# Rope tables on GpSimd, and a mixer's first chunks cut down to what the scan reads

## The chip, the cores and the metric

One core of a Trainium2 chip runs the whole program in one launch. The metric is the device time of one execution in microseconds (us). The kernel before takes 1905.51 us, the median of 3 runs (1904.94 to 1906.81). A change counts as seen here from about 0.2% on, 3.8 us.

## What is computed

A decoder trunk of two layers over 512 positions, width 1024, in float32. Each layer has a mixer, cross-attention into 256 memory tokens, and a gated MLP with a short convolution. Only the mixer's head matters here:

```python
h = rmsnorm(x, norm_mix[i])
z, xbc, dt_raw, c_q, c_kv, k_rope = jnp.split(h @ w_in[i], IN_SPLITS, axis=-1)
xbc = jax.nn.silu(causal_dwconv(xbc, ssm_conv_w[i], ssm_conv_b[i]))   # width 4
dt = jax.nn.softplus(dt_raw + dt_bias[i])                              # 16 heads
y = ssd_scan(xs, dt, a, bm, cm) + xs * d_skip[i][:, None]              # needs cumsum(dt * a)
q = rmsnorm(c_q, q_norm) @ w_uq ;  q_pe = apply_rope(q[..., 64:], cos, sin)
kv = rmsnorm(c_kv, kv_norm) @ w_ukv ;  k_pe = apply_rope(k_rope, cos, sin)
```

The tables are the cosine and sine of position times inverse frequency, the same for both layers.

## The kernel before

Activations lie transposed, features on the 128 partitions and the 512 positions along the row. Each float32 product is three matmuls of rounded halves (high by high, high by low, low by high; lines 168 to 170 in `mm3`). A weight tile of 128x1024 is loaded by SyncE into `wraw`; ScalarE rounds it to `whi` (line 107) and, as a rule, GpSimd subtracts to get `wlo` (line 108). There are three buffers of each, and the pair is made two tiles ahead. One **chunk** is 24 matmuls against one such pair: one column block of 128 features of a projection.

The mixer of a layer begins with six chunks (`latent_q`, `latent_kv`, and one that holds dt and the rope keys, `dtk`). A short run of 128x64 steps on VectorE (lines 415 to 430) makes the softplus `dt` and `w`, which is dt times a. Then 24 chunks follow in four groups of six (`inproj`), and attention's chunks. A loop gives each chunk a position, 0 to 23 for `inproj`. After each one, it takes a step of three coroutines:

- `front()`, the head: `rq` and `rk`, reciprocal roots of the latent norms (`rstd_cols`: four transposes on TensorE, a reduction on VectorE, a power on GpSimd in line 273, a product on VectorE in line 275); in layer 0 `rope_tables()`; rope keys `kpe`; query scales `csqa`, `csqb` (transposes by `bcast`, line 282); the normed key latents `ckh`, `ckl`; then the cumulative sums `acs` (two matmuls, lines 460 and 461, copied to SBUF in line 462), their transpose on TensorE (line 470) and its way through DRAM, `scr`.
- `scans`, one `ssd(g)` for each group, which start at the positions 5, 10, 16 and 21 and read `scr`, `acs`, `dt`.
- `memory()`, from position 12.

An `inproj` chunk of the convolved kind is followed by these steps: VectorE scales the bank (line 485), ScalarE makes the last tap and bias (492), VectorE adds three taps (494, three times), ScalarE takes the tanh (495), VectorE finishes (496).

TensorE's instructions stand in the order in which the program is written. The order on the other engines is chosen when the kernel is built, by a list scheduler, and is fixed from then on: each engine takes its instructions strictly one after the other.

## Time and profile before

| what | value |
|---|---|
| median of 3 runs | 1905.51 us |
| the profiled execution, its own time | 1904.88 us |
| its span, first to last instruction | 1903.2 us |
| TensorE busy | 1867.0 us, 98% |
| VectorE, ScalarE, GpSimd busy | 1035.5, 950.2, 885.7 us |
| mean granted TensorE clock | 0.995 |

The span is what the trace covers; some 1.7 us of the execution's own time lie outside it. Busy time of TensorE is modelled and includes matmuls that run at half clock. With an engine at 98%, the interesting part is the other 2%: where it stands still, and what it waits for there.

### The profile page before, as it was taken

Reading aid. Unit: us, or ns where it says so; the run is one execution under the profiler, and the core shown is the slowest. Engines: PE = TensorE matmul, PEld = TensorE weight load, DVE = VectorE, ACT = ScalarE, POOL = GpSimd, SP = SyncE. Lnnn points to the kernel's source line nnn. Section 1 sums busy time; section 2 is a strip of 40 time slices with the busy share of each in tenths; the row PEclk is TensorE's granted clock in tenths of the full one; section 3 lists DMA queues with packets and bytes.
Section 4 is the critical chain, followed back from the end, with each engine's and each line's share of the span. In section 5 each row is a group of like instructions: output and inputs, shape, how many; then the busy total and the mean of one; then the engine's idle time right before and its main releaser. Section 6 shows DMA issues by size and latency. Waiting matters only on the chain.

```text
span 1903.2 us, 24916 instructions
## 1 busy us (share of the span) xinstructions
PE 1867.0 (98%) x9264; PEld 1572.9 (83%) x9264; DVE 1035.5 (54%) x1967; ACT 950.2 (50%) x1694; POOL 885.7 (47%) x563
## 2 busy tenths in 40 slices
PE   8799999999999999999999999999999999999998
PEld 6588889988888888888887888898888888888887
DVE  5867788843343555541138777887334445555312
ACT  5366588843345444433235557888334544444321
POOL 5345455655416444433354454555553354444232
PEclk9899999999999999999999999999999999999999
DMA  5233311232213322233223332113322122332322
GB/s 168 68 122 111 103 51 59 93 125 94 91 34 109 100 100 97 92 97 100 92 100 101 113 110 82 58 62 122 110 91 88 50 96 98 100 100 90 102 91 84
DMA packets 56025, 178.47 MB, mean 94 GB/s; under 512 B 6368, under 2 KB 9312, under 8 KB 55904
## 3 DMA queue, kind: packets, MB, share of 16 engines
q1 hardware_dynamic: 49984, 166.32, 26.4%
q10 hardware_dynamic: 5920, 10.55, 1.7%
q8 instruction: 73, 1.20, 0.3%
q14 instruction: 48, 0.39, 0.1%
HBM read 174.69 MB, written 2.16 MB: 93 GB/s over the span
## 4 chain that ended last, share of the span: by engine, by line
PE 93%; DVE 2%; issue 1%; ACT 1%; POOL 1%; DMA 1%; SPq 0%; POOLq 0%; DVEq 0%; ACTq 0%
PE ps L168 28%; PE ps L170 28%; PE ps L169 28%; PE ps L728 2%; PE ps L709 1%; PE ps L583 1%; POOL wlo L108 1%; PE ps L589 1%; PE ps L562 1%; ACT whi L107 0%; DVE u L162 0%; PE ps L932 0%; PE ps L519 0%; PE ps L515 0%; PE ps L731 0%
## 5 line engine op out<-in xcount | busy, mean ns | idle before, releaser
L108 POOL TENSOR_TENSOR wlo<-wraw,whi 128x1024 fp32r<-128x1024 f32 (+1 forms) x290 | 679.1, 2343 | 855.7 <-ACT whi L107 836.6
L168 PE MATMUL ps<-u,whi 128*128 128x512 f32 (+1 forms) x2326 | 898.7, 386 | 7.7 <-ACT whi L107 5.1
L170 PE MATMUL ps<-u,wlo 128*128 128x512 f32 (+1 forms) x2326 | 890.0, 383 | 0.8 <-POOL wlo L108 0.6
L169 PE MATMUL ps<-u,whi 128*128 128x512 f32 (+1 forms) x2326 | 889.7, 383 | 0.0
L107 ACT ACTIVATE whi<-wraw 128x1024 fp32r<-128x1024 f32 (+2 forms) x319 | 328.2, 1030 | 494.7 <-PE ps L169 391.3
L168 PEld LDWEIGHTS ps<-u,whi 128*128 128x128 f32 x2326 | 438.9, 189 | 90.8 <-ACT whi L107 5.1
L170 PEld LDWEIGHTS ps<-u,wlo 128*128 128x128 f32 x2326 | 438.7, 189 | 87.3 <-POOL wlo L108 1.4
L169 PEld LDWEIGHTS ps<-u,whi 128*128 128x128 f32 x2326 | 439.2, 189 | 82.0 <-DVE u L165 0.7
L162 DVE TENSOR_TENSOR u<-ps,u 128x512 fp32r<-128x512 f32 (+2 forms) x236 | 137.2, 612 | 105.4 <-ACT u L159 104.7
L159 ACT ACTIVATE u<-ps 128x512 fp32r<-128x512 f32 (+2 forms) x236 | 117.7, 540 | 120.7 <-DVE ps L1021 98.4
L1017 DVE SCALAR_TENSOR_TENSOR u<-ps,small,u 128x510 f32<-128x510 f32 (+1 forms) x176 | 131.3, 749 | 74.7 <-ACT u L1015 71.7
L1010 DVE TENSOR_TENSOR ps<-ps,u 128x512 f32<-128x512 f32 x88 | 61.4, 700 | 109.9 <-PE ps L170 101.6
L301 POOL TENSOR_TENSOR u<-u,u 128x512 f32<-128x512 f32 (+1 forms) x82 | 102.5, 1251 | 37.0 <-ACT u L300 29.5
L108 DVE TENSOR_TENSOR wlo<-wraw,whi 128x1024 fp32r<-128x1024 f32 (+1 forms) x29 | 32.5, 1119 | 139.5 <-ACT whi L107 139.5
L697 POOL TENSOR_SCALAR u<-u,rs 128x512 f32<-128x512 f32 (+3 forms) x128 | 66.8, 537 | 79.7 <-DVE rs L696 75.0
L849 DVE TENSOR_TENSOR ps<-ps,u 128x512 f32<-128x512 f32 x32 | 22.4, 699 | 99.1 <-PE ps L170 99.1
L695 ACT ACTIVATE u<-ps,nm 128x512 f32<-128x512 f32 (+3 forms) x128 | 66.3, 524 | 18.1 <-DVE nm L692 12.1
L168 PE MATMUL ps<-u,u 128*128 128x512 f32 (+1 forms) x224 | 73.1, 326 | 0.9 <-ACT u L695 0.9
L170 PE MATMUL ps<-u,u 128*128 128x512 f32 (+1 forms) x224 | 72.1, 322 | 0.0
L169 PE MATMUL ps<-u,u 128*128 128x512 f32 (+1 forms) x224 | 72.0, 321 | 0.0
L494 DVE SCALAR_TENSOR_TENSOR u<-ps,half,u 128x509 f32<-128x509 f32 (+2 forms) x96 | 70.4, 742 | 1.2 <-ACT u L492 0.7
L1015 ACT ACTIVATE u<-ps,small 128x512 f32<-128x512 f32 x88 | 66.7, 760 | 1.7 <-DVE ps L1010 1.5
(193 smaller groups left out, 1769.3 us busy)
## 6 DMA issues: line engine op xcount, KB each, us to landing
wraw<-in_w_up SPq DMA_DIRECT2D x88, 512.0 KB, 3.4
wraw<-in_w_in SPq DMA_DIRECT2D x59, 512.0 KB, 3.5
wraw<-in_w_out SPq DMA_DIRECT2D x32, 512.0 KB, 3.4
wraw<-in_w_down SPq DMA_DIRECT2D x32, 512.0 KB, 3.4
u<-scr ACTq DMA_DIRECT2D x32, 256.0 KB, 4.6
wraw<-in_w_mk SPq DMA_DIRECT2D x16, 512.0 KB, 3.4
wraw<-in_w_mv SPq DMA_DIRECT2D x16, 512.0 KB, 3.4
wraw<-in_w_mq SPq DMA_DIRECT2D x16, 512.0 KB, 3.4
```

The source lines that it names most:

```text
L107: A.activation(hi[:, c], raw[:, c], AF.Copy)
L108: eng.tensor_tensor(lo[:, c], raw[:, c], hi[:, c].bitcast(F32), ALU.subtract)
L159: A.activation(hi, src, AF.Copy)
L162: (leng or V).tensor_tensor(lo, src, hi.bitcast(F32), ALU.subtract)
L168: T.matmul(o, lh, rh, start=start, stop=False)
L169: T.matmul(o, lh, rl, start=False, stop=False)
L170: T.matmul(o, ll, rh, start=False, stop=stop)
L301: (eng or G).tensor_tensor(self.acc, self.acc, sq, ALU.add)
L494: V.scalar_tensor_tensor(r_[:, d:], acc[:, :S - d], cw(3 - d), r_[:, d:], ALU.mult, ALU.add)
L697: G.tensor_scalar(p_[:, :n], p_[:, :n], rs[:, i:i + 1], 1.0, ALU.mult, ALU.mult)
L1015: A.activation(y, acc, AF.Identity, scale=fw(2), bias=par(layer, "ffn_b", ch))
L1017: V.scalar_tensor_tensor(y[:, d:], acc[:, :S - d], fw(2 - d), y[:, d:], ALU.mult, ALU.add)
```

## The change

- `rope_tables()` runs on GpSimd and ScalarE and not on VectorE. A fused multiply-add of VectorE becomes two instructions on GpSimd. It is called ahead of the second `latent_kv` chunk and not behind `rk`.
- `front()` makes `rq` and `rk` at the same positions as before, then only `acs` and its transpose, at their old positions 3 and 4. The rope keys come at position 8, the key latents at 9, the query scales at 12.
- The key tiles are built behind the second group of `inproj` and not behind the first.

```diff
     def rope_tables():
         ang, rnd, tab = unit(), unit(), unit()
-        V.tensor_copy(ang, posi)
-        V.tensor_scalar(ang, ang, rc[:, 0:1], None, ALU.mult)
+        G.tensor_copy(ang, posi)
+        G.tensor_scalar(ang, ang, rc[:, 0:1], None, ALU.mult)
...
         for cc in (c1, c2, c3):
-            V.scalar_tensor_tensor(ang, rnd, -cc, ang, ALU.mult, ALU.add)
+            G.tensor_scalar(tab, rnd, -cc, None, ALU.mult)
+            G.tensor_tensor(ang, ang, tab, ALU.add)
...
         A.activation(tab, ang, AF.Sin)
-        V.tensor_scalar(tab, tab, rc[:, 2:3], None, ALU.mult)
+        G.tensor_scalar(tab, tab, rc[:, 2:3], None, ALU.mult)
         G.memset(csa[0:64], 1.0)
-        V.tensor_copy(csa[64:128], tab[64:128])
-        V.tensor_copy(csb[0:64], tab[0:64])
+        A.copy(csa[64:128], tab[64:128])
+        A.copy(csb[0:64], tab[0:64])
...
         if layer == 0:
             prepare()
+            rope_tables()
         latent_kv(1)
...
             rk = rstd_cols(cks.acc, KVL, rx)
-            if layer == 0:
-                rope_tables()
-            kro, ksh = unit(), unit()
-            V.tensor_tensor(kro[64:128], dtk[64:128], csa[64:128], ALU.mult)
-            A.copy(ksh[64:96], kro[96:128])
-            V.tensor_tensor(kpe[64:96], kro[64:96], ksh[64:96], ALU.add)
-            A.copy(kpe[0:32], kpe[64:96])
-            yield
-            pq = bcast(rq)
-            V.tensor_tensor(csqa, pq, csa, ALU.mult)
-            V.tensor_tensor(csqb, pq, csb, ALU.mult)
-            yield
-            pk = bcast(rk)
-            for i in range(2):
-                n_ = unit()
-                V.scalar_tensor_tensor(n_, ckr[i], par(layer, "kv_norm", i), pk, ALU.mult, ALU.mult)
-                h_, l_ = unit(F32R), unit(F32R)
-                split(h_, l_, n_)
-                ckh.append(h_)
-                ckl.append(l_)
+            yield
+            yield
             yield
...
             A.dma_start(scr, acsT)
+            yield
+            yield
+            yield
+            yield
+
+            kro, ksh = unit(), unit()
+            V.tensor_tensor(kro[64:128], dtk[64:128], csa[64:128], ALU.mult)
+            A.copy(ksh[64:96], kro[96:128])
+            V.tensor_tensor(kpe[64:96], kro[64:96], ksh[64:96], ALU.add)
+            A.copy(kpe[0:32], kpe[64:96])
+            yield
+            pk = bcast(rk)
+            for i in range(2):
+                n_ = unit()
+                V.scalar_tensor_tensor(n_, ckr[i], par(layer, "kv_norm", i), pk, ALU.mult, ALU.mult)
+                h_, l_ = unit(F32R), unit(F32R)
+                split(h_, l_, n_)
+                ckh.append(h_)
+                ckl.append(l_)
+            yield
+            yield
+            yield
+            pq = bcast(rq)
+            V.tensor_tensor(csqa, pq, csa, ALU.mult)
+            V.tensor_tensor(csqb, pq, csb, ALU.mult)
             yield
...
-                if g == 0:
+                if g == 1:
                     key_tiles()
```

Three places of the order, all in layer 0. On GpSimd, from the weight pair of the third `inproj` chunk on; before:

```order
L108 TENSOR_TENSOR wlo_561<-wraw_479,whi_560 128x1024
L301 TENSOR_TENSOR u_344<-u_344,u_433 128x512
L273 TENSOR_TENSOR rstd_476<-tiny_471,mhalf 128x4
L108 TENSOR_TENSOR wlo_607<-wraw_558,whi_606 128x1024
L273 TENSOR_TENSOR rstd_528<-tiny_523,mhalf 128x4
L108 TENSOR_TENSOR wlo_663<-wraw_604,whi_662 128x1024
```

and now, where `wlo_558` is that third chunk's, and `wlo_597`, `wlo_636` the fourth's and fifth's:

```order
L108 TENSOR_TENSOR wlo_558<-wraw_503,whi_557 128x1024
L248 TENSOR_TENSOR u_400<-u_400,u_402 128x512
L302 TENSOR_TENSOR u_344<-u_344,u_457 128x512
L251 TENSOR_SCALAR u_400<-u_400,phs 128x512
L274 TENSOR_TENSOR rstd_500<-tiny_495,mhalf 128x4
L252 TENSOR_SCALAR u_400<-u_400 128x512
L254 TENSOR_SCALAR u_402<-u_402,rc 128x512
L108 TENSOR_TENSOR wlo_597<-wraw_555,whi_596 128x1024
L274 TENSOR_TENSOR rstd_552<-tiny_547,mhalf 128x4
L108 TENSOR_TENSOR wlo_636<-wraw_594,whi_635 128x1024
```

Ten more instructions of the tables (a cast, seven TENSOR_SCALARs, two TENSOR_TENSORs) stand ahead of `wlo_558`, behind the second chunk's pair; the powers of `rq` (`rstd_500`) and `rk` (`rstd_552`) stand between and behind the rest.

On ScalarE, from the last step of dt's exponentials on; before:

```order
L419 ACTIVATE dt_22_148<-dt_22_148 128x64
L107 ACTIVATE whi_606<-wraw_558 128x1024
L492 ACTIVATE u_510<-ps_485,half 128x512
L495 ACTIVATE ps_485<-u_510 128x512
L107 ACTIVATE whi_662<-wraw_604 128x1024
L252 ACT_TABLE_LOAD
L252 ACTIVATE u_533<-u_531 128x512
```

and now:

```order
L253 ACTIVATE u_402<-u_400 128x512
L107 ACTIVATE whi_596<-wraw_555 128x1024
L256 COPY csa<-u_402 64x512
L257 COPY csb<-u_402 64x512
L501 ACTIVATE u_534<-ps_509,half 128x512
L504 ACT_TABLE_LOAD
L504 ACTIVATE ps_509<-u_534 128x512
L107 ACTIVATE whi_635<-wraw_594 128x1024
```

The sine (`L252`, now `L253`) has moved ahead of the fourth chunk's `whi`, and the table load for the tanh stands ahead of the first chunk's tanh, which stands ahead of the fifth chunk's `whi`.

On VectorE, the last instructions ahead of `acs`; before:

```order
L452 SCALAR_TENSOR_TENSOR u_654<-u_431,small,ps_643 128x512
L496 SCALAR_TENSOR_TENSOR u_635<-ps_610,u_635 128x512
L485 TENSOR_TENSOR ps_666<-ps_666,u_387 128x512
L162 TENSOR_TENSOR u_657<-u_654,u_656 128x512
L462 COPY acs_152<-ps_699 128x64
```

and now:

```order
L494 TENSOR_TENSOR ps_600<-ps_600,u_387 128x512
L503 SCALAR_TENSOR_TENSOR u_625<-ps_600,half,u_625 128x511
L503 SCALAR_TENSOR_TENSOR u_625<-ps_600,half,u_625 128x510
L503 SCALAR_TENSOR_TENSOR u_625<-ps_600,half,u_625 128x509
L505 SCALAR_TENSOR_TENSOR u_625<-ps_600,u_625 128x512
L494 TENSOR_TENSOR ps_639<-ps_639,u_387 128x512
L446 COPY acs_152<-ps_672 128x64
```

Only the steps of the first three chunks and the scaling of the fourth are left ahead of it; keys, latents, scales and tables are gone from there. The lines of the changed kernel are later by up to nine: 485, 492, 494, 495, 496 are 494, 501, 503, 504, 505.

## Rows read from the trace of the kernel before

**Rows 1.** Waits of TensorE: line waited for, us in total, times, longest.
```profile
PE ps L470 <- DVE acs L462: 10.7, 1, 10.7
```

**Rows 2.** Timeline of TensorE, layer 0: start, us, engine, line, [idle before <- releaser].
```profile
62.61 0.39 PE L170 MATMUL ps<-u,wlo 128*128 128x512 f32 x1
65.49 0.62 PE L282 MATMUL ps<-ident,rstd 128*128 128x128 f32 x4 [2.49 <-DVE rstd L275]
77.13 0.39 PE L170 MATMUL ps<-u,wlo 128*128 128x512 f32 x1
88.19 0.42 PE L470 MATMUL ps<-ident,acs 128*64 128x128 f32 x1 [10.67 <-DVE acs L462]
```

**Rows 3.** Windows: stretch, then busy us of PE, PEld, DVE, ACT, POOL; PEclk.
```profile
57.00:88.30 31.30, 18.14 (x87) 14.57 (x85) 29.23 (x49) 14.27 (x18) 10.90 (x5) 0.88 0.16 57
95.00:130.00 35.00, 35.00 (x195) 29.39 (x194) 26.26 (x44) 22.38 (x42) 14.74 (x10) 1.00 0.31 106
```

**Rows 4.** Timeline of TensorE, layer 1.
```profile
1011.52 0.62 PE L282 MATMUL ps<-ident,rstd 128*128 128x128 f32 x4 [2.95 <-DVE rstd L275]
1025.02 0.48 PE L168 MATMUL ps<-u,whi 128*128 128x512 f32 x1
```

**Rows 5.** Groups of GpSimd by line and shape: count, busy us, mean ns of one.
```profile
L108 POOL TENSOR_TENSOR wlo<-wraw,whi 128x1024 fp32r<-128x1024 f32 x258 | 619.9, 2405 | 709.6 <-ACT whi L107 698.7 <-PE ps L265 8.0 <-PE ps L583 2.3
L301 POOL TENSOR_TENSOR u<-u,u 128x512 f32<-128x512 f32 x75 | 97.4, 1298 | 36.7 <-ACT u L300 29.5 <-PE ps L589 5.6
L697 POOL TENSOR_SCALAR u<-u,rs 128x512 f32<-128x512 f32 x32 | 22.3, 698 | 69.2 <-DVE rs L696 69.2
L273 POOL TENSOR_TENSOR rstd<-tiny,mhalf 128x4 f32<-128x4 f32 x14 | 15.0, 1071 | 19.0 <-DVE tiny L271 18.3
```

**Rows 6.** Timeline of GpSimd, layer 0, the second chunk's pair.
```profile
38.86 2.39 POOL L108 TENSOR_TENSOR wlo<-wraw,whi 128x1024 fp32r<-128x1024 f32 x1 [0.30 <-ACT whi L107]
```

**Rows 7.** Timelines of ScalarE, layer 0.
```profile
69.82 0.63 ACT L252 ACTIVATE u<-u 128x512 f32<-128x512 f32 x1 [5.68 <-DVE u L251]
...
76.80 0.78 ACT L492 ACTIVATE u<-ps,half 128x512 f32<-128x512 f32 x1
77.48 1.04 ACT L107 ACTIVATE whi<-wraw 128x1024 fp32r<-128x1024 f32 x1
80.08 1.28 ACT L495 ACT_TABLE_LOAD   x1 [1.56 <-DVE u L494]
81.38 0.60 ACT L495 ACTIVATE ps<-u 128x512 f32<-128x512 f32 x1
```

**Rows 8.** Timelines of VectorE and GpSimd where they meet, later in layer 0.
```profile
178.74 0.60 DVE L812 COPY rm<-rstd 128x2 f32<-128x2 f32 x1 [0.23 <-POOL rstd L273]
178.67 2.41 POOL L549 TENSOR_SCALAR_AFFINE_SELECT u<-u 128x512 f32<-128x512 f32 x4
...
280.48 0.16 DVE L696 RECIPROCAL rs<-rs 128x1 f32<-128x1 f32 x1 [0.40 <-ACT u L695]
279.31 1.86 POOL L108 TENSOR_TENSOR wlo<-wraw,whi 128x768 fp32r<-128x768 f32 x1 [4.24 <-ACT whi L107]
```

**Rows 9.** Timeline of VectorE, layer 0: steps of dt, and the first chunk's scaling.
```profile
52.38 2.28 DVE L427 TENSOR_SCALAR dt<-dt 128x64 f32<-128x64 f32 x1
...
56.65 0.22 DVE L426 TENSOR_TENSOR dt<-dt,dt 128x64 f32<-128x64 f32 x1
56.91 0.20 DVE L427 TENSOR_SCALAR dt<-dt 128x64 f32<-128x64 f32 x1
57.02 0.69 DVE L485 TENSOR_TENSOR ps<-ps,u 128x512 f32<-128x512 f32 x1
```

**Rows 10.** Groups of VectorE by line and shape: count, busy us, mean ns.
```profile
L494 DVE SCALAR_TENSOR_TENSOR u<-ps,half,u 128x511 f32<-128x511 f32 x32 | 23.8, 745 | 0.8 <-ACT u L492 0.7
```

**Rows 11.** Timelines of VectorE and GpSimd, layer 1.
```profile
1009.08 2.29 DVE L275 TENSOR_TENSOR rstd<-rstd,rstd 128x4 f32<-128x4 f32 x1 [0.65 <-POOL rstd L273]
1009.02 2.33 POOL L108 TENSOR_TENSOR wlo<-wraw,whi 128x1024 fp32r<-128x1024 f32 x1
```

More of the change, by code (lines that the diff above doesn't have):

```diff
@@ L236, in rope_tables @@
         ang, rnd, tab = unit(), unit(), unit()
-        V.tensor_copy(ang, posi)
-        V.tensor_scalar(ang, ang, rc[:, 0:1], None, ALU.mult)
+        G.tensor_copy(ang, posi)
+        G.tensor_scalar(ang, ang, rc[:, 0:1], None, ALU.mult)
         magic = 12582912.0
-        V.tensor_scalar(rnd, ang, 1.0 / (2 * math.pi), rc[:, 1:2], ALU.mult, ALU.add)
-        V.tensor_scalar(rnd, rnd, magic, None, ALU.add)
-        V.tensor_scalar(rnd, rnd, magic, None, ALU.subtract)
+        G.tensor_scalar(rnd, ang, 1.0 / (2 * math.pi), rc[:, 1:2], ALU.mult, ALU.add)
+        G.tensor_scalar(rnd, rnd, magic, None, ALU.add)
+        G.tensor_scalar(rnd, rnd, magic, None, ALU.subtract)
         c1 = 6.28125
@@ L246, in rope_tables @@
         for cc in (c1, c2, c3):
-            V.scalar_tensor_tensor(ang, rnd, -cc, ang, ALU.mult, ALU.add)
+            G.tensor_scalar(tab, rnd, -cc, None, ALU.mult)
+            G.tensor_tensor(ang, ang, tab, ALU.add)
         phs = cp.tile([P, 1], F32, name="phs")
-        V.tensor_scalar(phs, rc[:, 1:2], 2 * math.pi, None, ALU.mult)
-        V.tensor_scalar(ang, ang, phs, None, ALU.add)
-        V.tensor_scalar(ang, ang, 3.1415925, -3.1415925, ALU.min, ALU.max)
+        G.tensor_scalar(phs, rc[:, 1:2], 2 * math.pi, None, ALU.mult)
+        G.tensor_scalar(ang, ang, phs, None, ALU.add)
+        G.tensor_scalar(ang, ang, 3.1415925, -3.1415925, ALU.min, ALU.max)
         A.activation(tab, ang, AF.Sin)
-        V.tensor_scalar(tab, tab, rc[:, 2:3], None, ALU.mult)
+        G.tensor_scalar(tab, tab, rc[:, 2:3], None, ALU.mult)
         G.memset(csa[0:64], 1.0)
-        V.tensor_copy(csa[64:128], tab[64:128])
-        V.tensor_copy(csb[0:64], tab[0:64])
+        A.copy(csa[64:128], tab[64:128])
+        A.copy(csb[0:64], tab[0:64])
         G.memset(csb[64:128], 1.0)
```

## The prediction

> **What bounds the kernel now.** First the page: TensorE is busy 98% of the span, so only what it waits for can be won back. Then its waits: one single wait of 10.7 us stands far above the rest, the transpose of `acs` behind VectorE's copy in line 462 [rows 1]. The timeline of TensorE puts it in the head of layer 0's mixer, between the fifth and the sixth `inproj` chunk, 77.36 to 88.19; another one of 2.49 us lies at 65.49, where the transposes of `rk` wait for line 275 [rows 2]. Layer 1 has only the second kind, 2.95 us at 1011.52; its sixth chunk starts at 1025.02, with no wait for `acs` [rows 4]. Third the windows: from 57.0 to 88.3 VectorE is busy 29.23 of 31.30 us, while GpSimd has 10.90 and ScalarE 14.27 [rows 3]. So a queue on VectorE is the cause: tables, keys, scales and latents stand ahead of `acs`, which TensorE needs first. That is the most the change can win: 10.7 + 2.5 + 2.95, some 16 us, and what a lowered clock costs behind the waits (the granted clock averages 0.88 in that stretch [rows 3]).
>
> **What the change takes away.** The two transposes for `rq` and `rk` leave the head, so both waits at line 282 go. On VectorE all table, key, scale and latent steps go from ahead of `acs`. TensorE's instructions are the same in number: two groups of four transposes, 0.38 us each, come back in later chunks, 0.76 us a layer, which has to be taken off what the sixth chunk's earlier start shows. The wlo and whi of one chunk now depend on other neighbours; that is where the cost lies.
>
> **GpSimd's chain, layer 0.** The second chunk's wlo ends at 38.86 + 2.39 = 41.25 as before [rows 6]. Behind it stand the cast, seven TENSOR_SCALARs and two TENSOR_TENSORs. A TENSOR_SCALAR of 128x512 takes 0.698, a TENSOR_TENSOR of 128x512 1.298 [rows 5]. No row shows a cast on GpSimd, nor a dependent chain there; I take the cast at 0.70, as the row that it is nearest to (one input, one output, same shape), the ends being 0.60, the share of one of the four selects in 2.41 us [rows 8], and 1.30. So 0.70 + 7 x 0.70 + 2 x 1.30 = 8.2, to 49.45; the third chunk's wlo, 2.4, to 51.85 (TensorE wants it at about 57); then 1.30 + 1.30 + 0.70 to 55.15; the power of `rq`, 1.07, to 56.2; line 252, 0.70, to 56.9. The sine waits for that on ScalarE: 0.63 to 57.5, and only then comes the fourth chunk's whi, 1.05 to 58.6 [rows 7], and its wlo to 61.0. The fourth chunk can start at 62.5 (the third ends at 62.84 [rows 2], less the 0.35 of the transposes that no longer lie ahead of it). So the tables themselves are hidden, with 1.5 us to spare.
>
> **VectorE beside it.** The 22 small steps of dt run in 0.26 us from start to start when GpSimd is quiet, but one took 2.28 while a wlo ran [rows 9]. A copy of two columns took 0.60 beside four selects in a row, and a reciprocal 0.16 beside a wlo [rows 8]: the first waited for the end of one GpSimd instruction, the second for nothing, and the copy got in between two of GpSimd's. The Trainium skill ("SBUF — State Buffer", section "SBUF: two separate sides") has a rule for this: VectorE and GpSimd share one pair of ports as an exclusive lock, taken by VectorE operations with two SBUF inputs or in a two-port mode, and whoever comes second waits for the whole instruction of the other. The rule speaks against this change: nearly every step of dt is of those kinds, so all of them would be held, and the sum is the one below; were they as free as the reciprocal, it would be that of the first rival. The copy and the 2.28 us agree with it. By the rows I count one small step for each GpSimd instruction as long as GpSimd runs without a pause, from 46 to 57. That is ten steps or so; the product for `rq` among them, line 276, waits besides for the power, to 56.2. Two more get through while ScalarE takes the sine and some two before the fourth wlo starts; that blocks VectorE to 61.0. The eight that are left take 2.1, to 63.1; the first chunk's scaling 0.65, `rk`'s reduction and six small steps 1.7, to 65.45; `rk`'s power 1.07 and its product, to 66.65; three taps, 2.0, to 68.65. In the kernel before the scaling ran at 57.02 [rows 9].
>
> **What is late next.** On ScalarE the table load, 1.28, waits for the taps, then the tanh, 0.60, to 70.5, and only behind it stands the fifth chunk's whi: 71.6, its wlo 74.0. TensorE is there at 68.5, so it waits some 5 us for a weight pair. It does not set the end: VectorE finishes the first chunk at 71.2, and the second and third take a round each of scaling 0.65, ScalarE 0.78, taps 2.0, tanh 0.60, finish 0.69 [rows 7, 10], 4.8 with the handing over; so 80.8, scaling of the fourth 0.65, `acs` 81.7. TensorE, done with the fifth chunk at 79, waits for that, 2.7 us. The sixth chunk starts at 81.8 and not at 88.26: 6.4 less the 0.76 of transposes moved behind it, **5.7 us** in layer 0. Of 13.2 us of waits some 7.7 stay, now for a weight pair and for `acs`.
>
> **Layer 1.** No tables here. `rk`'s product ran at 1009.08 and lost 2.29 us to the wlo that began 0.06 earlier [rows 11]. Two steps of 0.69 leave VectorE ahead of it, so it comes 1.4 us earlier, likely behind the same wlo: 1009.9. Three small steps and a finish, 1.3; two rounds, 9.6; scaling and copy, 0.85: `acs` at 1021.6. TensorE, without its wait of 2.95 and the transposes, is there at about 1020.1 (the fourth chunk from 1008.6, two chunks of 5.6, cumulative sums 0.36). The sixth chunk starts at 1021.7 and not at 1025.02; less 0.76: **2.6 us**. Without the collision with the wlo it would be 4.2 at most.
>
> **Later chunks.** Seven microseconds of VectorE work a layer move into positions 8 to 12. I cost this at nothing: from 95 to 130 VectorE is busy 26.26 of 35.00 us [rows 3], of which the key tiles, 2.8, move on too. Keys and scales are not read before position 24. If that cover were gone, whatever of the seven does not fit would show as a wait for a bank.
>
> **Sum.** 5.7 + 2.6 = 8.3. The profiled execution took 1904.88, 0.63 below the median; 1904.9 - 8.3 = 1896.6. I forecast **1896.5**.
>
> **The rivals.**
> - *VectorE is not held up.* If dt's small steps slip through as the reciprocal did [rows 8], the first chunk's scaling stays at 57.02 and only `rk`'s power behind the fourth wlo counts: 61.0 + 1.07, product and taps 64.3, load and tanh 66.2, finish 66.9, two rounds 76.5, `acs` 77.3. Layer 0 wins 88.2 - 77.3 - 0.76 = 10.1, layer 1 4.2: **1890.5**. For it: the reciprocal, and nothing here shows that only one small step passes in a gap. Against it: the step of 2.28 us.
> - *GpSimd's chain is a few microseconds longer.* Each small step of VectorE that gets in between takes up to 0.26 from GpSimd, 14 times, 3.6 us; line 276 and the fourth wlo move by as much. Layer 0 then wins 2.1, the sum is 4.7: **1900.2**.
> - *Slower.* The power on 128x4 takes 1.07 us where a TENSOR_SCALAR on 128 times as many columns takes 0.70 [rows 5]: some GpSimd instructions have a large fixed price. If the 14 of the tables carry 1 us more each, ScalarE's sine, and behind it all whi, come 14 us later, and TensorE stands still for the fourth pair from 62.5 to 75: `acs` at 95.7, layer 0 loses 8.3, layer 1 still wins 2.6: **1910.6**. It decides from 8.3 us on, that is from 0.6 us more per instruction.
> - *The wait moves on.* The moved seven microseconds meet the first scans and TensorE waits there for a bank, in both layers: the gain is given back, **1905**. Against it stand the nearly nine idle microseconds of VectorE in that stretch.
>
> **How the numbers follow.** Chances: forecast 0.45, not held up 0.25, longer chain 0.16, slower 0.07, moved on 0.07. A difference under 0.2%, 3.8 us, can't be told from none. Faster: the forecast, the first rival, and 0.11 of the second, 0.81. Same: the rest of the second and most of the last, 0.11. Slower: 0.08. The range, 1889 to 1902.5, takes in the first two rivals, with 0.1 us less per TENSOR_SCALAR at its lower end, and leaves out the others and the luckiest of the first, two chances in ten. The half clock behind the waits is left at what it cost before; it moves either end by about 1 us.
>
> **What would show it.** In the changed profile: (1) no wait at the moved transposes; (2) 14 GpSimd instructions of 0.70 and 1.30, the sine starting at about 57; (3) VectorE's dt steps stretched to the length of GpSimd's, the first scaling at 63 rather than 57; (4) a wait of some 5 us for `whi` and `wlo` at the fifth chunk, with `acs` copied near 81.7; (5) layer 1's wait for `rk` replaced by 1 to 2 us for `acs`. The forecast is wrong if the sine starts after 60 or the scaling at 57, or if TensorE waits anywhere from position 8 on.

## The result and the profile after

The changed kernel is **slower**: 1916.98 us, the median of 5 executions (1913.80 to 1917.52), against 1905.16 for the kernel before (5 executions beside it). The ratio is 1.0057, with an interval of 1.0046 to 1.0069. The forecast was 1896.5, with a range up to 1902.5. The profiled execution of the changed kernel took 1917.13, its span 1915.4.

Where the time went is best read from a few fixed points of TensorE: its first matmul, and the first transposes of a group's outputs for the scan (line 515, now 524; "px" below). TensorE's order of chunks is the same in both kernels, so the stretches between these points can be compared one by one. All are differences of two start times in TensorE's timeline.

| stretch of TensorE | before | after | change | forecast |
|---|---|---|---|---|
| first matmul to px of the first group, layer 0 | 95.48 | 96.62 | +1.14 | -6.4 |
| px of the first to px of the second group | 34.18 | 34.61 | +0.43 | +0.38 |
| second to third group, layer 0 | 39.82 | 44.27 | +4.45 | +0.38 |
| to px of the first group of layer 1 (its head lies in here) | 861.45 | 857.64 | -3.81 | -3.3 |
| first to second group, layer 1 | 34.16 | 34.60 | +0.44 | +0.38 |
| second to third group, layer 1 | 39.61 | 49.25 | +9.64 | +0.38 |

The changes sum to +12.3, and the span grew by 12.2. So only layer 1's head did what was forecast; three stretches went wrong. Each stretch is read from one profiled execution, and TensorE's granted clock makes it scatter: among the kernels below, the five that leave this head of layer 0 as it is show it at 94.79 to 96.62, and the four that leave layer 1's second group as it is show the last stretch at 47.54 to 49.25. The head's +1.14 against the kernel before is within that; its 7.5 against the forecast is not.

The waits of TensorE in the changed kernel name the places (line waited for, us in total, times, longest; its own leader before is [rows 1]):

```profile
PE ps L266 <- POOL u L302: 8.6, 1, 8.6
PE ps L454 <- DVE acs L446: 4.8, 2, 3.1
PE ps L598 <- ACT u L580: 4.8, 2, 3.3
PE ps L598 <- ACT u L573: 2.1, 1, 2.1
```

**Layer 0's head.** TensorE's timeline, to be laid beside [rows 2]:

```profile
59.53 1.12 PE L266 MATMUL ps<-ident,u 128*128 128x128 f32 x4 [8.64 <-POOL u L302]
...
88.05 0.42 PE L454 MATMUL ps<-ident,acs 128*64 128x128 f32 x1 [3.07 <-DVE acs L446]
```

The wait of 10.67 for `acs` is down to 3.07, but a new one of 8.64 stands ahead of it: the transposes for `rk` wait for the squares of the key latents, line 302, a GpSimd instruction. GpSimd's timeline shows why (start, us):

```profile
41.61 1.58 POOL L238 TENSOR_SCALAR u<-u,rc 128x512 f32<-128x512 f32 x1
43.30 0.70 POOL L240 TENSOR_SCALAR u<-u,rc 128x512 f32<-128x512 f32 x1
44.08 1.51 POOL L241 TENSOR_SCALAR u<-u 128x512 f32<-128x512 f32 x1
45.68 1.50 POOL L242 TENSOR_SCALAR u<-u 128x512 f32<-128x512 f32 x1
47.26 1.50 POOL L247 TENSOR_SCALAR u<-u 128x512 f32<-128x512 f32 x1
...
53.13 1.49 POOL L247 TENSOR_SCALAR u<-u 128x512 f32<-128x512 f32 x1
54.70 2.34 POOL L108 TENSOR_TENSOR wlo<-wraw,whi 128x1024 fp32r<-128x1024 f32 x1
57.00 1.26 POOL L248 TENSOR_TENSOR u<-u,u 128x512 f32<-128x512 f32 x1
58.22 1.26 POOL L302 TENSOR_TENSOR u<-u,u 128x512 f32<-128x512 f32 x1
59.47 1.57 POOL L251 TENSOR_SCALAR u<-u,phs 128x512 f32<-128x512 f32 x1
61.00 1.04 POOL L274 TENSOR_TENSOR rstd<-tiny,mhalf 128x4 f32<-128x4 f32 x1
62.02 0.62 POOL L252 TENSOR_SCALAR u<-u 128x512 f32<-128x512 f32 x1
```

Two things are to be seen. A TENSOR_SCALAR with two operations (lines 240 and 252) takes 0.62 to 0.70 us; one with a single operation (the second operand `None`) takes 1.49 to 1.58 on the same 128x512, and eight of the ten are of that kind. And the squares and `rq`'s power (line 274) stand behind nearly all of it. ScalarE and VectorE stand still meanwhile; one row of each, with the idle time in brackets:

```profile
62.67 0.63 ACT L253 ACTIVATE u<-u 128x512 f32<-128x512 f32 x1 [15.07 <-POOL u L252]
```

```profile
48.21 0.22 DVE L428 TENSOR_TENSOR dt<-dt,dt 128x64 f32<-128x64 f32 x1
62.08 0.57 DVE L276 TENSOR_TENSOR rstd<-rstd,rstd 128x4 f32<-128x4 f32 x1 [13.64 <-POOL rstd L274]
...
65.06 2.38 DVE L428 TENSOR_TENSOR dt<-dt,dt 128x64 f32<-128x64 f32 x1
...
68.56 0.69 DVE L494 TENSOR_TENSOR ps<-ps,u 128x512 f32<-128x512 f32 x1
...
87.78 0.21 DVE L446 COPY acs<-ps 128x64 f32<-128x64 f32 x1
```

VectorE's first scaling (line 494, before 485) starts at 68.56 and not at 57.02 [rows 9], and `acs` is copied at 87.78.

The waits are not all of it. Windows of the whole head and of its stretches at half clock, first of the kernel before, then of the changed one (length, TensorE busy; PEclk is the third number from the end):

```profile
5.10:100.60 95.50, 80.64 (x346) 64.22 (x347) 69.86 (x118) 44.63 (x68) 39.18 (x19) 0.95 0.35 120
80.90:91.00 10.10, 2.81 (x8) 2.23 (x9) 9.40 (x16) 5.45 (x10) 2.40 (x2) 0.50 0.31 104
```

```profile
5.10:101.80 96.70, 82.95 (x338) 65.58 (x339) 51.43 (x93) 40.97 (x62) 56.69 (x34) 0.91 0.34 115
52.90:63.10 10.20, 3.57 (x11) 2.99 (x12) 0.95 (x4) 0.43 (x1) 9.57 (x8) 0.50 0.15 51
87.10:93.80 6.70, 5.75 (x14) 4.52 (x15) 4.99 (x13) 3.63 (x7) 3.38 (x2) 0.50 0.29 102
```

TensorE stood still for 14.9 us of the head before and for 13.8 now, a little less. But it was busy 83.0 us for 80.6, with the eight moved transposes gone from it. The clock fell to 0.50, 1.2 GHz, while it stood for the squares, and again while it stood for `acs`: 16.9 us at half clock, for 10.1 before.

**The second group's scan.** Both layers have it; layer 1 is the worse. TensorE, then ScalarE of the changed kernel, where line 515 issues the loads of the group's decay rows, 562 takes their exponentials, 573 and 580 copy the states:

```profile
1097.25 0.72 PE L598 MATMUL ps<-u,u 128*128 128x128 f32 x2 [2.10 <-ACT u L573]
1101.29 1.71 PE L598 MATMUL ps<-u,u 128*128 128x128 f32 x4 [3.31 <-ACT u L580]
```

```profile
1074.70 2.94 ACTq L515 DMA_DIRECT2D u<-scr  x4
...
1084.18 4.79 ACT L562 ACTIVATE u<-u,nacs 128x128 f32<-128x128 f32 x16
1089.00 1.89 ACT L621 CAST u<-u 32x512 fp32r<-32x512 f32 x3
...
1095.94 0.60 ACT L504 ACTIVATE ps<-u 128x512 f32<-128x512 f32 x1 [1.72 <-DVE u L503]
...
1096.83 0.37 ACT L573 COPY u<-ps 128x256 f32<-128x256 f32 x1 [0.28 <-issue]
1099.92 1.06 ACT L107 ACTIVATE whi<-wraw 128x1024 fp32r<-128x1024 f32 x1 [2.72 <-DMA wraw<-in_w_in]
1100.88 0.35 ACT L580 COPY u<-ps 128x256 f32<-128x256 f32 x1
```

The same instructions of the kernel before (lines 506, 553, 564, 571):

```profile
1068.81 2.11 ACTq L506 DMA_DIRECT2D u<-scr  x4
...
1076.21 2.74 ACT L553 ACTIVATE u<-u,nacs 128x128 f32<-128x128 f32 x9
...
1086.69 0.36 ACT L564 COPY u<-ps 128x256 f32<-128x256 f32 x1
...
1088.86 0.36 ACT L571 COPY u<-ps 128x256 f32<-128x256 f32 x1
```

TensorE reaches this group 2.72 us later than before (1072.90 and 1070.18). Take that off, and the loads are issued 3.2 us later, the exponentials start 5.3 later, the first state copy comes 7.4 later, the second 9.3. VectorE shows what stands between exponentials and states now, the key tiles (line 622) and the query scales (480, 481):

```profile
1085.56 0.69 DVE L563 TENSOR_TENSOR u<-u,ps 128x512 f32<-128x512 f32 x1 [4.20 <-ACT u L562]
...
1089.79 2.77 DVE L622 TENSOR_TENSOR u<-u,u 32x512 fp32r<-32x512 f32 x4
...
1093.26 0.68 DVE L480 TENSOR_TENSOR u<-ps,csa 128x512 f32<-128x512 f32 x1
...
1098.21 0.41 DVE L576 TENSOR_TENSOR u<-ps,cd 128x256 f32<-128x256 f32 x1
```

The first state copy stands in ScalarE's order behind the tanh of line 504, which waited 1.72 us for VectorE's taps (line 503), and these stand behind the key tiles and between the scales. The second copy stands behind the rounding of a weight tile at 1099.92, which by the profile waited 2.72 us for the tile's load. SyncE, which had waited for GpSimd to finish an earlier `wlo`, issued its next loads only here:

```profile
1095.81 2.63 SPq L99 DMA_DIRECT2D wraw<-in_w_in  x2
```

In the kernel before, two roundings stood ahead of the second copy, at 1086.95 and 1087.91, and waited for nothing. No run moves this rounding alone.

Behind the first of the two waits, 5.41 us together, TensorE's granted clock falls. Two windows of the changed kernel:

```profile
1097.40:1107.60 10.20, 6.76 (x18) 5.11 (x19) 8.53 (x16) 3.87 (x6) 3.05 (x2) 0.50 0.54 191
1070.00:1085.00 15.00, 15.00 (x80) 12.79 (x79) 8.80 (x17) 6.89 (x13) 8.01 (x7) 1.00 0.41 141
```

For 10.2 us TensorE ran at 1.2 GHz and not at 2.4; so 5.41 us of waits cost 9.3, the moved transposes taken off. In layer 0 it waited 1.9 us and ran at half clock from 162.2 to 165.5, which cost 4.1.

### The profile page after: what moved, and what is told of

It reads as the page before. It is cut to its first block, busy times and chain, and to the rows that moved or that the text cites. A ratio compares the mean times of both kernels' runs of the same rounds, so it can differ in the third digit from the quotient of the medians.

```text
span 1915.4 us, 24924 instructions
## 1 busy us (share of the span) xinstructions
PE 1874.3 (98%) x9264; PEld 1577.6 (82%) x9264; DVE 1025.6 (54%) x1953; ACT 951.7 (50%) x1696; POOL 902.0 (47%) x578
## 4 chain that ended last, share of the span: by engine, by line
PE 86%; DVE 4%; POOL 3%; ACT 3%; DMA 2%; issue 2%; ACTq 0%; SPq 0%; POOLq 0%; DVEq 0%
PE ps L168 27%; PE ps L170 27%; PE ps L169 27%; PE ps L737 2%; POOL wlo L108 1%; PE ps L718 1%; DVE u L503 1%; DMA wraw<-in_w_in 1%; ACT whi L107 1%; PE ps L598 1%; PE ps L592 0%; ACT u L562 0%; PE ps L571 0%; PE ps L941 0%; PE ps L740 0%
## 5 line engine op out<-in xcount | busy, mean ns | idle before, releaser
L302 POOL TENSOR_TENSOR u<-u,u 128x512 f32<-128x512 f32 (+1 forms) x82 | 102.3, 1249 | 34.2 <-ACT u L301 26.6
L704 ACT ACTIVATE u<-ps,nm 128x512 f32<-128x512 f32 (+3 forms) x128 | 66.2, 523 | 18.2 <-DVE nm L701 12.3
```

Of the source, the lines that this page charges most:

```text
L302: (eng or G).tensor_tensor(self.acc, self.acc, sq, ALU.add)
```

## The experiments

The theory drawn from this profile had two parts. **Head**: GpSimd's tables are longer than counted, because of the one-operation form, and the squares are queued behind them. **Scan**: the moved steps make the second group's state copies late. Rivals: the hold-up of VectorE makes the head long; the tables alone, or the late loads alone, make the scan late. The table has every run, with the stretches of the table above (first px, second to third group in layer 0, layer 1's head, second to third group in layer 1); ratios are against the kernel before on the same chip, with their intervals. Where TensorE waits in a stretch, differences under 2 us are not read, because of the scatter named above.

| kernel | head 0 | scan 0 | head 1 | scan 1 | median us | ratio |
|---|---|---|---|---|---|---|
| before | 95.48 | 39.82 | 861.45 | 39.61 | 1905.16 | |
| after | 96.62 | 44.27 | 857.64 | 49.25 | 1916.98 | 1.0057 (1.0046 to 1.0069) |
| two operations | 89.51 | 42.67 | 857.65 | 47.54 | 1910.87 | 1.0025 (1.0016 to 1.0034) |
| tables as before | 87.84 | 44.27 | 857.59 | 49.21 | 1907.23 | 1.0005 (0.9996 to 1.0014) |
| front as before | 98.90 | 39.82 | 860.81 | 39.60 | 1907.77 | 1.0010 (1.0001 to 1.0019) |
| key tiles late | 95.66 | 41.65 | 859.35 | 45.31 | 1914.49 | 1.0044 (1.0027 to 1.0061) |
| tables later | 79.47 | 50.84 | 857.64 | 48.93 | 1913.74 | 1.0046 (1.0032 to 1.0061) |
| loads early | 95.92 | 42.03 | 857.63 | 44.55 | 1910.19 | 1.0022 (1.0011 to 1.0032) |
| spread | 87.96 | 40.29 | 858.91 | 40.07 | 1896.48 | 0.9951 (0.9937 to 0.9966) |
| spread, tables at six | 80.47 | 40.81 | 858.87 | 40.07 | 1903.47 | 0.9990 (0.9980 to 1.0000) |
| spread, one operation | 93.34 | 40.29 | 858.96 | 40.07 | 1903.91 | 0.9990 (0.9980 to 0.9999) |
| tables with the latents | 90.31 | 40.28 | 858.82 | 40.07 | 1899.12 | 0.9966 (0.9953 to 0.9978) |
| sine cut off | 79.65 | 42.39 | 858.93 | 40.07 | 1896.51 | 0.9953 (0.9938 to 0.9967) |
| sine cut off, angles at six | 80.53 | 42.18 | 859.00 | 40.09 | 1896.02 | 0.9951 (0.9936 to 0.9966) |
| scales late | 96.52 | 42.18 | 857.59 | 46.52 | 1912.41, one execution | |
| latents early | 95.54 | 45.50 | 858.07 | 46.64 | 1914.80, one execution | |
| loads and tiles | 94.79 | 40.26 | 858.43 | 40.05 | 1903.90, one execution | |

The first to second group of layer 0 takes 34.2 to 34.6 us in all but four: 41.73 with the tables later, 47.75 with the tables at six, 36.22 and 38.53 in the two with the sine cut off.

### The form of the table steps

The six statements of 128x512 with one operation (eight instructions) get a second that changes nothing; the order on every engine stays, and so does the one small step for `phs`.

```diff
-        G.tensor_scalar(ang, ang, rc[:, 0:1], None, ALU.mult)
+        G.tensor_scalar(ang, ang, rc[:, 0:1], 1.0, ALU.mult, ALU.mult)
...
-        G.tensor_scalar(rnd, rnd, magic, None, ALU.subtract)
+        G.tensor_scalar(rnd, rnd, magic, 1.0, ALU.subtract, ALU.mult)
```

> The changed kernel, with a second operation (times 1.0) in the eight large and one small TENSOR_SCALARs of the tables that had one operation only; the order on every engine stays the same. Theory: a TENSOR_SCALAR with one operation takes 1.5 us on GpSimd and one with two takes 0.70 (lines 240 and 252 of the changed kernel have two and take 0.70 and 0.62). Then all tables' TENSOR_SCALARs take 0.62 to 0.75, the sine starts some 6 us earlier, near 56.5, the wait of 8.6 us for the squares of the key latents falls to about 3, and the time falls by 5 to 8 us to about 1910.5. Rival: the 1.5 us come from the dependence of one step on the last, or from VectorE's hold on the shared port; then the instructions keep their 1.5 us and the time stays at 1917.

The time, 1910.87, is what the theory said. The head took 89.51 us, 7.1 less. GpSimd's rows:

```profile
42.04 0.70 POOL L238 TENSOR_SCALAR u<-u,rc 128x512 f32<-128x512 f32 x1
...
44.34 1.94 POOL L242 TENSOR_SCALAR u<-u 128x512 f32<-128x512 f32 x1
46.37 0.62 POOL L247 TENSOR_SCALAR u<-u 128x512 f32<-128x512 f32 x1
...
54.83 1.26 POOL L302 TENSOR_TENSOR u<-u,u 128x512 f32<-128x512 f32 x1
```

All but one fall to 0.62 to 0.70; the pair subtract and multiply (line 242) takes 1.94, and in the spread run below, as add of the negative and multiply, 0.62. The form is thus shown to be a cost of the head. The eight took 6.6 us for 12.2; TensorE stood still for 9.1 us of the head and not 13.8, and the rest of the 7.1 us is clock (a mean of 0.96 in the head for 0.91). But line 302 still ends only at 56.09, and TensorE waits 4.68 us for it and not the 3 that were expected: the order costs too.

### Each half of the change alone

"Tables as before" keeps the moved steps and gives the tables back to VectorE, behind `rk`; "front as before" keeps the new tables and undoes all moves.

```diff
-            prepare()
-            rope_tables()
+            prepare()
...
             rk = rstd_cols(cks.acc, KVL, rx)
+            if layer == 0:
+                rope_tables()
```

> The changed kernel with the tables back on VectorE at their old place, ahead of the cumulative sums; keys, latents and scales stay at positions 8, 9 and 12. Theory: the tables on GpSimd cost layer 0's head, and the moved steps cost the scan of the second group in both layers (TensorE waits 2 to 5.5 us for the states there, then runs at half clock). Then the wait for the squares goes, the wait for the cumulative sums is some 4 to 5 us rather than 10.7, the scan's waits stay in both layers (1.9 and 5.4 us), and the time is about 1909. Rival: the tables are at fault for all; then the scan's waits go too and the time is about 1898.

> The changed kernel's tables (GpSimd, called early), with keys, scales, latents and key tiles at their old places. Theory: the wait for the squares of the key latents stays at 8 to 9 us, the cumulative sums come behind tables and keys later than before, the second group's scan shows no wait in either layer, and layer 1 is as in the kernel before. Time 1910 to 1916. Rival: the moved steps are at fault for all; then 1905 or less.

The moved steps alone shorten layer 0's head by 7.6 us and layer 1's by 3.9, and lose 4.45 and 9.60 in the two scans, with the waits there unchanged, as the theory of that run said; the time can't be told from that of the kernel before. The tables alone lengthen the head by 3.4 and leave both scans as they were. Their time, 1907.77, lies between the theory's 1910 to 1916 and the rival's 1905: the wait for the squares came as expected, 8.63, but the one for `acs` shrank to 4.46, so TensorE stood still for 14.9 us of that head, as long as before, and what the head lost is lower clock (0.91 for 0.95). So the scan's loss belongs to the moved steps and not to the tables. The head shows that the two do not add: -7.6 and +3.4 would be -4.2, and together they gave +1.1. With the moves alone the head stands at 87.84; the tables on GpSimd then cost 8.8, since most of the long wait for `acs`, beside which their own wait was hidden in the run with the tables alone, is no longer there: 5.45 us of it are left with the moves alone, 3.07 in the change.

### What makes the second group late

"Key tiles late" builds them behind the fourth group (`if g == 3`). "Loads early" takes the first step of the second group's scan, its loads, two chunk positions earlier.

```diff
-                if pos >= START[g]:
+                if pos >= START[g] and not (g == 1 and pos == START[g]) or g == 1 and pos == START[g] - 2:
```

> The changed kernel with the key tiles behind the fourth group and not behind the second. Theory: their 2.8 us on VectorE and 2.5 us on ScalarE stand in front of the states of the second group's scan, so the waits for the state copies (1.9 us in layer 0, 5.4 in layer 1) shrink to 2 or less in sum and with them the half clock; the time falls by 5 to 9 us to about 1910. Rival: the late loads of that group's decay rows, put off by keys and latents, decide alone; then the waits stay and the time falls by 2 at most.

> The changed kernel with the first step of the second group's scan, its loads of the decay rows, two chunk positions earlier. Rival 'late loads': the second group's exponentials are late because these loads are issued behind waiting copies on ScalarE's queue (1074.70 for 1067 before, in layer 1); then the waits of TensorE for the state copies in layer 1 (2.1 and 3.3 us) fall to under 1.5 in sum and the half clock behind them goes: 1910 to 1913 us. Theory 'too much ahead of the state copies': the loads are no longer late but the key tiles and query scales still stand ahead of the state copies on VectorE and ScalarE, the waits keep over 3 us of their 5.4 in layer 1: 1915 to 1918.

Neither is the whole cause: of layer 1's 9.64 us, the early loads give back 4.70 and the late tiles 3.94, and of the 5.41 us of waits 2.41 and 3.12 are left. In their waits both lie between theory and rival; the early loads' time, 1910.19, is the one given for late loads. The late tiles missed their forecast of about 1910, at 1914.49: of the 6.6 us that they won in the scans 3.8 were lost again where attention runs, 1.7 us in layer 0's rest (859.35 for 857.64) and 2.1 behind layer 1's third group. In the run with early loads the exponentials start at 1077.95 and the state copies still come only at 1090.60 and 1095.05, behind key tiles at 1082.76 and scales. Three kernels that ran once each went after the rest.

> The changed kernel with the query scales alone moved, from the thirteenth to the seventeenth chunk position. From the second group's first px transposes to the third group's, layer 1 took 39.61 us before and 49.25 in the changed kernel. If the scales (two VectorE products directly ahead of the state products, and a group of transposes) are the last thing that makes the state copies late, the stretch falls to 42 us or less; if the late exponentials are, they would be late without the scales too, and it keeps 46 us or more. In between, both share it.

> The changed kernel with the key latents alone moved, from the tenth to the sixth chunk position. The copies of the latents' rounding stand ahead of the second group's load issues on ScalarE's queue. If they make the loads late, the loads are issued at 1067 to 1070 us as before (less the shift of layer 1) and the layer-1 stretch of 49.25 us falls to 44 or less, as with the loads issued two positions earlier (44.55); if not, it stays at 47 or more.

> The changed kernel with the second group's loads two positions earlier and the key tiles behind the third group. Alone these took 4.7 and 3.9 us off the layer-1 stretch of 49.25 us. If the two delays lie one behind the other on the same chain, both together bring it to 40 to 42 us, near the 39.61 of before; if each only uncovers the other, it stays at 44 or more.

Scales moved alone: 46.52, latents alone: 46.64, each some 2.7 less. The first is just on the side of the late exponentials (46 or more), the second between its two answers, and both are too near to what the same order scatters by to decide more than this: neither is the cause by itself. In layer 0 the latents' move did not help, 45.50. In all four runs that move one thing, what is left in layer 1 is mostly the wait for the second state copy (1.45 to 3.36 us), the one behind the weight rounding. Loads and tiles together (the tiles behind the third group): 40.05 and, in layer 0, 40.26, with no wait at line 598. Their single gains of 4.7 and 3.9 add up to 8.6 of the 9.2 that were there beyond the moved transposes. That fits a chain, by what the run was expected to show: late loads, late exponentials, then tiles and scales ahead of what the state copies wait for; taking two links out frees it. Head 0 of that run is still 94.79, and its 1903.90 is near the 1904.20 of the kernel before, which ran once beside it.

### Other places for the steps

"Tables later" calls the tables (two operations) at the sixth position and leaves the rest. "Spread": tables at the second position, behind the squares; latents at the sixth, keys at the eleventh, scales at the seventeenth, tiles with the third group. The next is the same with the tables at the sixth. "Spread, one operation" has the form of the change.

```diff
+            yield
+            if layer == 0:
+                rope_tables()
...
-                if g == 1:
+                if g == 2:
                     key_tiles()
```

> The two-operation table steps on GpSimd are taken out of layer 0's head and stand at the sixth chunk position, after the acs and its transpose; the other moved steps stay in the changed order (keys at the ninth, latents at the tenth, scales at the thirteenth, key tiles with the second group). If the head pays only for what stands ahead of the acs, TensorE's waits for the squares (4.68 us in the two-operation run) and for the acs (2.75) both fall under 1 us and the first px transposes come 6 to 7 us earlier than at 96.00; the scan's waits stay as in the changed kernel (1.9 us in layer 0, 5.2 to 5.4 in layer 1): 1904 to 1905 us. Rival: the tables and the sine then stand beside the second group's exponentials and add to the state copies' delay, the waits of the second group's scan in layer 0 go from 1.9 to 6 us or more: 1908 to 1911.

> Two-operation tables on GpSimd one chunk position behind the squares of the key latents, latents at the sixth position, keys at the eleventh, scales at the seventeenth, key tiles with the third group. If the second group's state copies were late because keys, latents, scales and key tiles all stand within a few positions ahead of them, spreading takes the waits in the second group's scan to under 1 us in both layers; with the squares ahead of the tables the wait for them (4.68 us) goes too and the acs waits 1 to 4 us: 1896 to 1902 us, faster than before. Rival: the steps only carry their delay along, and waits of 3 us or more turn up at the third or fourth group's scan or where the keys are used: 1905 to 1910.

> As the spread run, but the tables stand with the latents at the sixth position, behind the acs and its transpose. By the theory of two separate costs the head is free of tables (first px transposes near 89 to 91 us, 96.00 in the two-operation run) and the scan's waits stay under 1 us: 1893 to 1899 us. Rival: sine and tables beside the first two groups' exponentials delay the state copies of the first or second group by what the tables take on ScalarE and VectorE (a sine of 2.4 us and a change of its function table of 1.3 us, twice): waits of 3 to 6 us in layer 0's scan and 1898 to 1904 us.

> The spread run (1896.48 us) with the one-operation form of the six table steps put back, nothing else. Theory: the form costs 0.8 to 0.9 us for each of the eight instructions of 128x512 that have one operation, some 7 us of GpSimd's chain, and since ScalarE's queue stands behind the sine, TensorE waits that much longer in layer 0's head, where the spread run waited 4.6 us for a weight pair: 1901 to 1904 us. Rival: with the squares of the key latents ahead of the tables the chain has room, and the form costs under 1 us: 1896 to 1897.5.

The spread run is faster than both kernels, at 1896.48. Its scans are back at 40.3 and 40.1, 0.5 above before, about the moved transposes. In the head the wait for the squares is gone as its theory said, but TensorE waits for a weight pair (3.35 and 1.22 us) and not for `acs`. That the time equals the forecast's 1896.5 is chance: it is another order with other waits. The form of the table steps alone makes 5.4 us of its head (93.34 and 87.96), and 7.4 us of its time, as the theory of that run said. With the tables at the sixth position the head is free of them (79.47 and 80.47), but the time comes back at once: with the tables later, the next two stretches are 7.5 and 11.0 us longer than before, so that run's rival was right and too low. In the run "tables at six", TensorE and ScalarE:

```profile
105.16 2.12 PE L574 MATMUL ps<-u,u 128*128 128x256 f32 x4 [11.01 <-DVE u L548]
```

```profile
88.05 1.28 ACT L253 ACT_TABLE_LOAD   x1
99.27 0.63 ACT L253 ACTIVATE u<-u 128x512 f32<-128x512 f32 x1 [9.94 <-POOL u L252]
```

The sine stands ahead of the first group's tap and copy in ScalarE's fixed order, and the engine stands there for 9.94 us, until GpSimd has the angles. The time, 1903.47, is the rival's, but not for its reason: the sine itself takes 0.63 us and not the 2.4 of that text, and the cost is a single wait in the first group, with 0.3 us of waits in the second.

### The sine away from the angles

Cutting the function in two and giving the sine a bias column of zeros, made from a later chunk's output, moves it on ScalarE behind that chunk. "Tables with the latents" tries the opposite, the whole function ahead of the second query latent chunk.

```diff
-        A.activation(tab, ang, AF.Sin)
+        V.tensor_scalar(zb, gate, 0.0, None, ALU.mult)
+        A.activation(tab, ang, AF.Sin, bias=zb)
```

> The spread run with the sine cut off from the angles: GpSimd makes the angles where it did (62 to 78 us), and the sine is tied to the sixth inproj chunk's output by a bias column of zeros, so that ScalarE does not reach it before its argument is there. Theory: ScalarE's wait for the clamped angle (6.86 us, ahead of the third chunk's tanh) was what held the weight pair up; without it TensorE waits under 1.5 us in the head and the first px transposes come at 87 to 89 us for 93.18: 1890 to 1892.5 us. Rival: GpSimd's chain itself holds VectorE up in the head, the first px transposes come no earlier than 91, or the sine with its two table loads now delays the first group's exponentials: 1894 to 1898.

> As the run with the sine cut off, but the angles stand at the sixth position (GpSimd from 82 to 99 us) and the sine is tied to a chunk of the second group. Theory: the head is then free of tables, first px transposes at 86 to 87 us as in the run with tables at the sixth position, and the wait of 11.0 us at the first group's state products goes, since it was ScalarE standing at the sine 9.94 us: 1889 to 1891.5 us. Rival: the sine and its table loads, 4 us of ScalarE between the second group's loads and its exponentials, bring back waits of 2 us or more at the second group's scan: 1893 to 1898.

> The spread run with the two-operation tables called ahead of the second chunk of the mixer's query latents, so that GpSimd makes them between 13 and 40 us and the sine lies ahead of dt's exponentials. Theory: with no table step left in the first six inproj chunks, TensorE's wait for the weight pair (3.35 and 1.22 us near 84 us) goes, and the first px transposes come at 86.5 to 89 us for 93.18, with the later steps as they are: 1890 to 1893 us. Rival: in the latents' chunks the table steps stand ahead of a wlo or of squares that TensorE needs, or hold up VectorE's squares of x, and TensorE waits there 4 us or more: 1896 to 1902.

Both cut-off kernels have the head at 79.65 and 80.53, 8 us less than the spread run and a little less than their theories said, and yet its time, which lies in the rivals' ranges. What was won comes back in the first two groups: 36.22 and 38.53, 42.39 and 42.18, in many small waits of 0.4 to 1.0 us for the scan's products and state copies. Of 8.3 us 4.1 are given back in the first profile, of 7.4 us 6.3 in the other. The first profile's execution was the fastest of four: 1893.95 at a mean granted clock of 0.998, the others 1895.76 at 0.997 and 1897.25 and 1897.80 at 0.996. So the rest of what that kernel won goes with a lower clock in the other three; where it fell in them no trace shows. With the tables among the latents, TensorE waits for `rx`, whose power (line 274) now stands behind table steps in GpSimd's order (3.9 us of them, beside a `wlo` and two squares), from 35.6 us, when VectorE had done its part, to 44.39. TensorE, then GpSimd:

```profile
45.49 1.11 PE L283 MATMUL ps<-ident,rstd 128*128 128x128 f32 x4 [7.16 <-POOL rstd L274]
```

```profile
43.73 0.69 POOL L254 TENSOR_SCALAR u<-u,rc 128x512 f32<-128x512 f32 x1
44.39 1.04 POOL L274 TENSOR_TENSOR rstd<-tiny,mhalf 128x4 f32<-128x4 f32 x1
```

The rival of that run was right: 1899.12.

## Why the prediction was wrong

- **"GpSimd's chain, layer 0" failed first, by two steps.** The term 0.70 for a TENSOR_SCALAR was taken from a row of one line [rows 5] that has two operations; eight of the ten new ones have one, at 1.49 to 1.58. That is 6.6 us by the durations. Undoing it moved the head by 7.1 (5.4 in the spread order), of which 4.7 was TensorE standing still and the rest clock. The rival "Slower" had the right kind of cause, a price of the instruction, some 0.83 on eight instructions instead of 1 on fourteen, but was given 0.07.
- **The squares were not followed.** The prediction listed the second 1.30 behind the third wlo in the chain and asked only when the sine is ready. It did not ask who waits for line 302: the transposes for `rk`, which ran at 51.00 in the kernel before. Even with its own durations they would have come at 54.45. With the two-operation form, nearest to those durations, TensorE waited 4.68, in the change 8.64. "So the tables themselves are hidden, with 1.5 us to spare" was wrong for that reason alone.
- **"The half clock behind the waits is left at what it cost before" failed, and by more than the 1 us that was allowed for it.** The two points above cost 4.0 of the 7.5 us that the head missed: of its 13.2 us of waits 7.7 were to stay, and 11.7 came (8.64 for the squares, 3.07 for `acs`). Another 3.1 is TensorE's busy time: 2.3 more than before, where 0.76 less was due for the transposes, with 6.8 us more at half clock. In the scans 7.3 of the 13.3 us are waits, and some 5 are half clock by these rows: 1.6 in layer 0, where the run with two operations has the same waits without it, and 3.4 in layer 1, half of the 6.76 us that TensorE was busy from 1097.4 to 1107.6.
- **"VectorE beside it" counted too much, without harm.** One small step for each GpSimd instruction was expected from 46 to 57; nine went through between 46.2 and 48.4, in 0.15 to 0.55 us each, beside two TENSOR_SCALARs with one operation. Beside a wlo one took 2.38, as before [rows 9]. The Trainium skill ("SBUF — State Buffer", section "SBUF: two separate sides") states that of a GpSimd operation and a VectorE operation with two SBUF inputs or in a two-port mode, the second waits for the whole instruction of the first. That row agrees, and so do 1.31 us beside a TENSOR_TENSOR of 1.28 in the run with two operations; for the TENSOR_SCALARs of 1.5 the trace does not agree: the two-input product at 48.21 took 0.22 within one that ran from 47.26 to 48.76. It did not matter: VectorE stood at line 276 from 48.4 to 62.08, as the text said it would, to 56.2.
- **"What is late next" held in its mechanism.** `acs` was late because of VectorE's rounds behind a late first scaling; 19.2 us lie between that scaling and the copy of `acs`, for which the prediction had counted 18.6. With the tables where they were, the head shrank by 7.6 us, so moving keys, latents and scales does pay in the head; that this is near the 6.4 of the forecast, which had the tables on GpSimd, is chance.
- **"Layer 1" was right:** 3.3 us forecast for the stretch (the moved transposes fall behind it), 3.8 measured; the wait for `rk` went, and one of 1.75 us for `acs` came, where 1 to 2 had been said.
- **"Later chunks", cost at nothing, failed, and is the larger half.** The cover was read as a sum of idle time over 35 us of the first group [rows 3]. The steps went into the second group, and there the question is not how much is idle but what stands ahead of the state copies in VectorE's and ScalarE's fixed order. It cost 4.07 and 9.26 us beyond the transposes. TensorE waited there for copied states, not for a bank as the prediction would have it. "The wait moves on" named the place and was set at 8.3 us for both layers; with the half clock behind the waits it was 13.3.

The step sums: -8.2 forecast by stretches, +7.5 for the head, +13.3 for the scans, -0.5 for layer 1 give +12.1, and 12.2 were measured.

## What to carry to other kernels

A step that moves "into idle time" moves ahead of something: list what stands behind it on each engine in order, and ask which of those TensorE waits for next, rather than add up idle shares. Take an instruction's price from a row of the same form, number of operations included, and where two changes free one head, measure each alone, since a cover that one uses up is gone for the other.

## What the runs showed of the hardware

- On GpSimd a TENSOR_SCALAR of 128x512 in float32 takes 1.49 to 1.58 us with one operation and 0.61 to 0.71 with two, of which the second may be a multiplication by one. Subtract with multiply is the exception, 1.94; add of the negative with multiply takes 0.62. Eight rows with two operations took 0.95 to 1.16 while VectorE ran instructions of 128x512: four with the tables among the latents, two each with the tables and with the angles at the sixth position.
- A cast of 128x512 from int32 takes 0.61 to 0.63 us on GpSimd, and 1.05 beside VectorE's squares in the run with the tables among the latents; the prediction had no row for it.
- The same waits can cost a different time: 1.9 us of waits in layer 0's second group came with 3.3 us at half clock in the change and with none in the run with two operations, 44.27 and 42.67 us for the same order.
- Why small steps of VectorE pass beside the slow form of TENSOR_SCALAR and not beside a TENSOR_TENSOR was not tried by itself and stays open; so does how the small waits of the two cut-off kernels divide among the first group's instructions.
